# Reordering the hand-over from the output projection to the up projection

## The chip, the cores and the metric

The kernel runs on one core of one Trainium2 chip. The metric is the device time of one execution, in microseconds (us). Three runs of the kernel before gave 1262.51 to 1264.11 us, with a median of 1263.84 us.

## The reference

One decoder layer for 1024 tokens and a width of 1024, all in fp32:

```python
a = rmsnorm(h, g_mix[i]);  proj = a @ w_in[i]          # gated convolution and attention groups
h = h + jnp.concatenate([conv_out, attn], axis=-1) @ w_out[i]
m = rmsnorm(h, g_mlp[i])
h = h + jnp.square(jax.nn.relu(m @ w_up[i])) @ w_down[i]
gate = jax.nn.sigmoid(rmsnorm(h, g_ple[i]) @ w_ple_gate[i])
h = h + gate * (p[i] @ w_ple_proj[i]);  out = rmsnorm(h, g_final)
```

The change lies between the second line (the output projection, whose result is the new residual) and the fourth (`m @ w_up`, 1024 x 4096).

## The kernel before

**Number format.** Every fp32 operand of a matrix product is cut in two parts: *hi*, a cast on ScalarE (ACT, L904), and *lo*, the difference of operand and hi, a subtraction on VectorE (DVE, L908). A product takes three matmuls per 128-deep piece, in the order hi*hi, hi*lo, lo*hi. So the first matmul of a product needs only the hi part of the right operand, and the second needs its lo part.

**Output projection, second half.** Eight steps `tt`, one for each 128 tokens, with two halves of 512 columns each. `out_half(tt, dh)` records the 12 matmuls of one half (L158) and its *eviction*, the addition of the bank to the residual row on DVE (L725). A step also has: `norm_begin(tt)`, the sum of squares on ACT (L118) and two small instructions on GpSimd (POOL, L123 and L126) that give the row's factor `rs`; the store of the row to `h_d` by the SP queue; and, one step later, `m_row(tt)` (L1290), the normalised row, which waits for `rs`. Rows 0 to 3 of the normalised residual go out to `m_d` and come back in another layout (`row_back`, L1273), and four transposes on DVE (`turn_part`, L1279) put them into the four units of `turn_raw[0]`. Rows 4 to 7 are turned on TensorE (`turn_on_pe`, L1307), and ACT copies them (L1309) into `turn_raw[1]`.

**Up projection.** One level of a Strassen scheme. For each of 16 slabs `n` of 256 columns of `w_up` there are seven products, P1 to P7, of 12 matmuls each (L1016). Their right operands are blocks of the turned residual: P1 uses B11 and P2 uses B21 (the two halves of `turn_raw[0]`), P3 uses B22, and P5, P6, P7, P4 use the combinations T1 to T4, which DVE makes by subtraction (L842) before they are cut in hi and lo. The left operands of a slab are cut by `blocks_jobs` (for P1, P2, P4) and `sums_jobs` (for P5, P6, P7, P3). After its product, a bank goes through ACT: a copy into another bank (P1, L1046), a relu and a square (P2 and P4, L1021 and L1022), or a plain copy (P6 L1052, P7 L1056). With P2 to P4 the result goes to `hs_d`. In what follows, "P1(2)" is product P1 of slab 2.

**What sets the order.** Here PE, DVE, ACT and SP keep the order in which the code records their instructions. The cutting of operands is recorded as *jobs* in one queue. `pump(us)` adds `us` to a credit and runs jobs, each with a cost that the code states, while the credit is above zero; the credit never keeps more than 0.5. `begin_ahead` records the casts of the first two jobs of the queue early. Where a product's operand has not been cut yet, `up` runs jobs until it has:

```python
while name not in ups[n] or RIGHT[name] not in M:
    run_one()
```

Such *forced* jobs are recorded after everything that the product before put on ACT and DVE. Their costs are taken off the credit, so that the next pumps run fewer jobs.

Of the kernel before, what the change touches and what calls it, by code (L numbers as in the profile page):

```python
# [14 lines left out]
P = 128  # L15
# [46 lines left out]
def hybrid_layer_kernel(ctx: ExitStack, tc: tile.TileContext, x, p, g_mix, w_in, conv_w, g_conv_out,  # L62
                        g_attn_out, w_out, g_mlp, w_up, w_down, g_ple, w_ple_gate, w_ple_proj,
                        g_final, out):
    nc = tc.nc
    x, p, w_in, conv_w, w_out, w_up, w_down, w_gate, w_proj, out = (
        x[0], p[0, 0], w_in[0], conv_w[0], w_out[0], w_up[0], w_down[0], w_ple_gate[0], w_ple_proj[0], out[0])
# [639 lines left out]
    h1 = []  # L707
# [126 lines left out]
    def free(*us):  # L834
        for u in us:
            U.put(u, "W")
# [20 lines left out]
    jobs = deque()  # L857
# [20 lines left out]
    def begin_ahead():  # L878
        for j in list(jobs)[:AHEAD]:
            if j.act and (j.need is None or j.need.done) and len(U.free_q["W"]) > SPARE:  # L880
                j.begin()

    def run_one():
        j = jobs.popleft()
        j.begin()
        j.dve()
        j.done = True
        credit[0] -= j.cost
        begin_ahead()

    def pump(us):
        credit[0] += us
        begin_ahead()
        while jobs and credit[0] > 0:
            run_one()
        credit[0] = min(credit[0], 0.5)
# [41 lines left out]
    def sums_jobs(n, r, between=None):  # L938

        ops = ups[n]  # L940
        a11, a21 = r[0][0][:, :, 0:P], r[0][0][:, :, P:256]
        a12, a22 = r[1][0][:, :, 0:P], r[1][0][:, :, P:256]
        box = {}

        def s_sums():
            s = box["s"] = W(F32, (P, 2, 4, P))
            add(s[0][:, 0], a21, a22)
            sub(s[0][:, 1], s[0][:, 0], a11)

        def q_sums():  # L950
            q = box["q"] = W(F32, (P, 2, 4, P))
            sub(q[0][:, 0], a11, a21)
            sub(q[0][:, 1], a12, box["s"][0][:, 1])
            free(*r)

        made = {"s": job(s_sums, 1.4), "q": job(q_sums, 1.4)}
        if between:
            job(between, 0.0)
        for key, names in (("s", ("P5", "P6")), ("q", ("P7", "P3"))):
            def outs(key=key):  # L960
                box[key + "o"] = W(F32R, (P, 2, 4, P)), W(F32R, (P, 2, 4, P))
                return [u[0] for u in box[key + "o"]]

            def done(key=key, names=names):
                hi, lo = box[key + "o"]
                free(box[key])
                held = Held([hi, lo], 2)
                for i, name in enumerate(names):
                    ops[name] = ((lambda t, i=i: hi[0][:, i, t]), (lambda t, i=i: lo[0][:, i, t]), held)

            split_job(1.23, outs, lambda key=key: box[key][0], done, made[key])
# [3 lines left out]
    def block_jobs(name, raws_of, done=None, need=(None, None)):  # L975
        hi, lo = [], []
        for i in range(2):
            def outs():
                hi.append(W(F32R, (P, 2, HB)))
                lo.append(W(F32R, (P, 2, HB)))  # L980
                return hi[-1][0], lo[-1][0]

            def ready(i=i):
                if i == 1:
                    M[name] = ((lambda t: hi[t // 2][0][:, t % 2]), (lambda t: lo[t // 2][0][:, t % 2]), hi + lo)
                    if done:
                        done()
            split_job(1.23, outs, lambda i=i: raws_of()[i][0], ready, need[i])
# [44 lines left out]
    def up(n, name, us=2.6):  # L1033
# [54 lines left out]
        squares.extend(due)  # L1088
        if n == NP_ - 1:
            free(*M[RIGHT[name]][2])  # L1090
        pump(us)


    GP, NG = 2, NP_ // 2
# [166 lines left out]
    def out_half(tt, dh):  # L1261
        for _ in out_bank(y2, w2, tt, dh, TAGS[(2 * tt + dh) % 4]):
            pass
# [49 lines left out]
    with tc.manual_schedule(engines={mybir.EngineType.PE, mybir.EngineType.DVE, mybir.EngineType.Activation,  # L1313
# [2 lines left out]
        sums_jobs(1, raws[1])  # L1316
        for tt in range(8):
            out_half(tt, 0)
            if tt >= 1:
                m_row(tt - 1)  # L1320
            out_half(tt, 1)
            if 3 <= tt <= 6:
                if tt == 3:
                    turn_raw[0] += raw_units()
                turn_part(turn_raw[0], tt - 3, tt - 3, range(4))
            else:
                pump(3.6)
            norm_begin(h1, tt)
            nc.sync.dma_start(out=h_d[tt * P:(tt + 1) * P], in_=h1[tt][0])
            if 1 <= tt <= 4:  # L1330
                row_back(m_d, tt - 1)
            if tt == 6:
                while jobs:
                    run_one()
                r0 = turn_raw[0]
                block_jobs("B11", lambda: r0[0:2])
                block_jobs("B21", lambda: r0[2:4])
                begin_ahead()
        for a, b in y2 + w2:
            free(a, b)  # L1340
        blocks_jobs(2, raws[2])
        sums_jobs(2, raws[2])
        up(0, "P1", 2.4)
        m_row(7)
        free(grow)
        turn_on_pe(4)
        turn_on_pe(5)
        up(1, "P1", 2.6)
        turn_on_pe(6)
        turn_on_pe(7)  # L1350
        up(0, "P2", 0.0)
# [15 lines left out]
        t1, t2 = [], []  # L1367
        made = combine_jobs(sub, b12, b11, t1, lambda: free(*b11))
        block_jobs("T1", lambda: t1, need=made)
        made = combine_jobs(sub, b22, t1, t2, lambda: free(*t1))  # L1370
        block_jobs("T2", lambda: t2, need=made)
        t3 = list(b12)
# [280 lines left out]
```

## Time and profile before

| | |
|---|---|
| median of three runs | 1263.84 us |
| the profiled execution's own time | 1267.23 us |
| its span, first to last instruction | 1265.5 us |
| TensorE (PE) busy | 1213.4 us, 96% |
| DVE busy | 963.0 us, 76% |
| ACT busy | 628.5 us, 50% |
| mean granted TensorE clock | 0.986 |

All stretches below are microseconds from the start of the profiled span. Matmuls are pipelined and their ends are modelled, so the time of a product is read from start to start. An instruction's busy time on DVE or ACT overlaps that of the next by about 0.1 us.

### The profile page before, as it was taken

Reading aid. Unit: us, or ns where it says so; the run is one execution under the profiler, and the core shown is the slowest. Engines: PE = TensorE matmul, PEld = TensorE weight load, DVE = VectorE, ACT = ScalarE, POOL = GpSimd, SP = SyncE. Lnnn points to the kernel's source line nnn. Section 1 sums busy time; section 2 is a strip of 40 time slices with the busy share of each in tenths; the row PEclk is TensorE's granted clock in tenths of the full one; section 3 lists DMA queues with packets and bytes.
Section 4 is the critical chain, followed back from the end, with each engine's and each line's share of the span. In section 5 each row is a group of like instructions: output and inputs, shape, how many; then the busy total and the mean of one; then the engine's idle time right before and its main releaser. Section 6 shows DMA issues by size and latency. Waiting matters only on the chain.

```text
span 1265.5 us, 15613 instructions
## 1 busy us (share of the span) xinstructions
PE 1213.4 (96%) x5629; PEld 1004.0 (79%) x5629; DVE 963.0 (76%) x1367; ACT 628.5 (50%) x1049; POOL 236.4 (19%) x248
## 2 busy tenths in 40 slices
PE   8999999999998999899999999987899999999997
PEld 6788888878877788678888888865788888887786
DVE  3656898989989976678666766665889888886774
ACT  5445465555565432456545545563344444435543
POOL 3302544545448531000000000000000000002121
PEclk9999999999998999899999999989999999999899
DMA  9711011111122325124677776799787876567432
GB/s 361 221 34 44 28 31 34 35 34 34 34 67 89 128 81 203 66 92 164 231 271 251 262 276 249 276 302 325 243 258 228 264 239 214 190 207 229 134 101 99
DMA packets 152229, 209.71 MB, mean 166 GB/s; under 512 B 8004, under 2 KB 111448, under 8 KB 152152
## 3 DMA queue, kind: packets, MB, share of 16 engines
q1 hardware_dynamic: 151608, 207.67, 49.0%
q8 instruction: 44, 0.72, 0.2%
q10 hardware_dynamic: 544, 1.05, 0.2%
q14 instruction: 33, 0.27, 0.1%
HBM read 141.58 MB, written 67.11 MB: 165 GB/s over the span
## 4 chain that ended last, share of the span: by engine, by line
PE 51%; DVE 4%; DMA 3%; ACT 1%; issue 1%; SPq 0%; POOL 0%; POOLq 0%; DVEq 0%; ACTq 0%
PE ps_mm L1016 13%; PE ps_z L1016 12%; PE ps_av L1016 12%; PE ps_tr L1016 7%; PE ps_z L158 2%; PE ps_tr L158 2%; PE ps_mm L158 2%; PE ps_av L158 2%; DMA u<-hs_d 1%; DMA u<-h_d 1%; DVE u L1279 1%; DVE u L908 1%; DVE u L839 1%; DMA n_d<-u 1%; DVE u L842 1%
## 5 line engine op out<-in xcount | busy, mean ns | idle before, releaser
L158 PE MATMUL ps_mm<-u,u 128*128 128x512 f32 (+1 forms) x1464 | 366.4, 396 | 7.1 <-ACT u L904 2.6
L158 PEld LDWEIGHTS ps_mm<-u,u 128*128 128x128 f32 x1464 | 269.8, 190 | 62.3 <-ACT u L904 3.0
L908 DVE TENSOR_TENSOR u<-u,u 128x1024 fp32r<-128x1024 f32 (+2 forms) x214 | 231.2, 1101 | 43.1 <-ACT u L904 36.4
L904 ACT CAST u<-u 128x1024 fp32r<-128x1024 f32 (+2 forms) x214 | 195.0, 952 | 91.3 <-DVE u L842 20.4
L1016 PE MATMUL ps_z<-u,u 128*128 128x512 f32 x768 | 194.5, 396 | 14.4 <-DVE u L908 6.5
L1016 PE MATMUL ps_mm<-u,u 128*128 128x512 f32 x768 | 191.4, 391 | 6.5 <-DVE u L839 5.8
L1016 PE MATMUL ps_av<-u,u 128*128 128x512 f32 x744 | 186.1, 392 | 1.4 <-DVE u L908 1.4
L1016 PEld LDWEIGHTS ps_z<-u,u 128*128 128x128 f32 x768 | 145.9, 191 | 48.5 <-DVE u L908 8.3
L1016 PEld LDWEIGHTS ps_mm<-u,u 128*128 128x128 f32 x768 | 144.6, 189 | 38.2 <-DVE u L839 7.1
L1016 PEld LDWEIGHTS ps_av<-u,u 128*128 128x128 f32 x744 | 140.3, 189 | 31.8 <-DVE u L908 2.1
L123 POOL TENSOR_SCALAR me<-ms 128x1 f32<-128x1 f32 x24 | 10.3, 430 | 705.0 <-DVE u L839 619.6
L839 DVE TENSOR_TENSOR u<-ps_av,u 128x512 f32<-128x512 f32 x94 | 64.7, 689 | 81.8 <-PE ps_av L1016 48.1
L1016 PE MATMUL ps_tr<-u,u 128*128 128x512 f32 x408 | 102.0, 394 | 0.0
L1016 PEld LDWEIGHTS ps_tr<-u,u 128*128 128x128 f32 x408 | 77.6, 190 | 16.4
L603 POOL TENSOR_TENSOR u<-u,u 128x383 f32<-128x383 f32 (+5 forms) x72 | 72.7, 1012 | 94.4 <-DVE u L601 50.3
L842 DVE TENSOR_TENSOR u<-u,u 128x512 f32<-128x512 f32 (+1 forms) x120 | 84.2, 723 | 1.7
L620 ACT CAST u<-ps_tr 128x512 fp32r<-128x512 f32 (+1 forms) x80 | 43.5, 544 | 60.8 <-PE ps_tr L615 60.3
L645 PEld LDWEIGHTS ps_av<-u,u 128*128 128x128 f32 x320 | 50.2, 189 | 15.3 <-DVE u L621 9.0
L621 DVE TENSOR_TENSOR u<-ps_tr,u 128x512 fp32r<-128x512 f32 (+1 forms) x80 | 50.5, 632 | 14.8 <-ACT u L620 13.8
L596 DVE TENSOR_TENSOR_SCAN u<-u,floor 128x384 f32<-128x384 f32 (+2 forms) x64 | 58.4, 914 | 3.7 <-ACT u L588 3.6
L113 ACT CAST u<-u 128x1024 fp32r<-128x1024 f32 x42 | 43.9, 1054 | 33.9 <-DVE u L501 9.8
L645 PE MATMUL ps_av<-u,u 128*128 128x256 f32 (+1 forms) x320 | 52.9, 281 | 6.2 <-DVE u L621 6.1
(133 smaller groups left out, 1523.4 us busy)
## 6 DMA issues: line engine op xcount, KB each, us to landing
u<-in_w_down SPq DMA_DIRECT2D x56, 512.0 KB, 5.5
u<-hs_d SPq DMA_DIRECT2D x64, 448.0 KB, 5.8
hs_d<-u SPq DMA_DIRECT2D x48, 512.0 KB, 2.8
u<-in_w_up SPq DMA_DIRECT2D x32, 512.0 KB, 5.9
ws_d<-u SPq DMA_DIRECT2D x32, 512.0 KB, 2.8
u<-ws_d SPq DMA_DIRECT2D x32, 512.0 KB, 6.4
u<-in_w_in SPq DMA_DIRECT2D x24, 512.0 KB, 4.1
u<-in_x SPq DMA_DIRECT2D x16, 512.0 KB, 8.1
```

Of the source, the lines that this page charges most:

```text
L113: nc.scalar.copy(out=hi, in_=raw)
L158: nc.tensor.matmul(ps, a, b, start=(i == 0), stop=(i == n - 1))
L596: nc.vector.tensor_tensor_scan(out=rev, data0=rev, data1=floor[:, HB - (n - s0):][:, ::-1], initial=1.0, op0=ALU.mult, op1=ALU.max)
L603: (nc.vector if s0 > 0 and pr < 3 else nc.gpsimd).tensor_tensor(out=beta[:, s0:e], in0=beta[:, s0:e], in1=keep[:, s0 + 1:e + 1], op=ALU.mult)
L620: nc.scalar.copy(out=ah[:, :w], in_=tp[:, :w])
L621: nc.vector.tensor_tensor(out=al[:, :w], in0=tp[:, :w], in1=f32(ah[:, :w]), op=ALU.subtract)
L645: nc.tensor.matmul(av[:, t0:256], v, part[:, c0:c0 + 256 - t0], start=(j == 0 and part is ah), stop=(j == n - 1 and part is al))
L839: (eng or nc.vector).tensor_tensor(out=out, in0=a, in1=b, op=ALU.add)
L842: (eng or nc.vector).tensor_tensor(out=out, in0=a, in1=b, op=ALU.subtract)
L904: nc.scalar.copy(out=box["o"][0], in_=src())
L908: nc.vector.tensor_tensor(out=b, in0=src(), in1=f32(a), op=ALU.subtract)
L1016: nc.tensor.matmul(ps, a, b, start=(fresh and i == 0), stop=(i == n - 1), skip_group_check=not fresh)
```

## The change

It moves recorded instructions and changes none of them: the kernel after has the same instructions on each engine. Its parts:

1. In steps 3 to 6, the four transposes stand between the two evictions of a step, behind `m_row(tt - 1)`, instead of behind the second eviction.
2. The jobs of B11 and B21 are put at the head of the queue in step 6, before its second half, and the jobs that were left (the cutting of slab 1's sums) stay queued behind them. Before, those were all run first.
3. In step 7 two jobs (the lo parts of B11) run between the evictions, `m_row(6)` comes behind the second one, and `pump(3.6)` is gone.
4. The read of a turned row (`row_back`) is issued by SP ahead of the store of the step's residual row.
5. `up(1, "P1", None)` runs no pump behind P1(1).
6. `sums_jobs(2, ...)` is queued behind the jobs of T1 instead of ahead of them.

```diff
--- before.py
+++ after.py
@@ -1088,7 +1088,8 @@
         squares.extend(due)
         if n == NP_ - 1:
             free(*M[RIGHT[name]][2])
-        pump(us)
+        if us is not None:
+            pump(us)
 
 
     GP, NG = 2, NP_ // 2
@@ -1316,36 +1317,41 @@
         sums_jobs(1, raws[1])
         for tt in range(8):
             out_half(tt, 0)
-            if tt >= 1:
+            if tt == 7:
+                run_one()
+                run_one()
+            elif tt >= 1:
                 m_row(tt - 1)
-            out_half(tt, 1)
             if 3 <= tt <= 6:
                 if tt == 3:
                     turn_raw[0] += raw_units()
                 turn_part(turn_raw[0], tt - 3, tt - 3, range(4))
-            else:
+            if tt == 6:
+                r0 = turn_raw[0]
+                rest = list(jobs)
+                jobs.clear()
+                block_jobs("B11", lambda: r0[0:2])
+                block_jobs("B21", lambda: r0[2:4])
+                jobs.extend(rest)
+                begin_ahead()
+            out_half(tt, 1)
+            if tt == 7:
+                m_row(6)
+            if tt < 3:
                 pump(3.6)
             norm_begin(h1, tt)
-            nc.sync.dma_start(out=h_d[tt * P:(tt + 1) * P], in_=h1[tt][0])
             if 1 <= tt <= 4:
                 row_back(m_d, tt - 1)
-            if tt == 6:
-                while jobs:
-                    run_one()
-                r0 = turn_raw[0]
-                block_jobs("B11", lambda: r0[0:2])
-                block_jobs("B21", lambda: r0[2:4])
-                begin_ahead()
+            nc.sync.dma_start(out=h_d[tt * P:(tt + 1) * P], in_=h1[tt][0])
         for a, b in y2 + w2:
             free(a, b)
         blocks_jobs(2, raws[2])
-        sums_jobs(2, raws[2])
         up(0, "P1", 2.4)
         m_row(7)
         free(grow)
         turn_on_pe(4)
         turn_on_pe(5)
-        up(1, "P1", 2.6)
+        up(1, "P1", None)
         turn_on_pe(6)
         turn_on_pe(7)
         up(0, "P2", 0.0)
@@ -1367,6 +1373,7 @@
         t1, t2 = [], []
         made = combine_jobs(sub, b12, b11, t1, lambda: free(*b11))
         block_jobs("T1", lambda: t1, need=made)
+        sums_jobs(2, raws[2])
         made = combine_jobs(sub, b22, t1, t2, lambda: free(*t1))
         block_jobs("T2", lambda: t2, need=made)
         t3 = list(b12)
```

On DVE, steps 6 and 7 of the output projection (`u416` and `u417` are the residual rows 6 and 7, `u451` to `u454` the four units of `turn_raw[0]`, `u462` and later units of L1290/L1291 the normalised rows). Before:

```order
L725 TENSOR_TENSOR u416_4469<-ps_mm_4857,u416_4469 128x512
L1290 SCALAR_TENSOR_TENSOR u462_4871<-u396_4379,rs_4854,u429_4560 128x1024
L725 TENSOR_TENSOR u416_4469<-ps_z_4873,u416_4469 128x512
L1279 STREAM_TRANSPOSE u451_4746<-u459_4810 128x2x128
L1279 STREAM_TRANSPOSE u452_4747<-u459_4810 128x2x128
L1279 STREAM_TRANSPOSE u453_4748<-u459_4810 128x2x128
L1279 STREAM_TRANSPOSE u454_4749<-u459_4810 128x2x128
L908 TENSOR_TENSOR u444_4694<-u442_4690,u443_4693 128x1024
L908 TENSOR_TENSOR u447_4700<-u445_4696,u446_4699 128x1024
L725 TENSOR_TENSOR u417_4501<-ps_tr_4907,u417_4501 128x512
L1290 SCALAR_TENSOR_TENSOR u468_4921<-u416_4469,rs_4896,u429_4560 128x1024
L725 TENSOR_TENSOR u417_4501<-ps_av_4923,u417_4501 128x512
```

After:

```order
L725 TENSOR_TENSOR u416_4469<-ps_mm_4857,u416_4469 128x512
L1291 SCALAR_TENSOR_TENSOR u462_4871<-u396_4379,rs_4854,u429_4560 128x1024
L1280 STREAM_TRANSPOSE u451_4732<-u459_4809 128x2x128
L1280 STREAM_TRANSPOSE u452_4733<-u459_4809 128x2x128
L1280 STREAM_TRANSPOSE u453_4734<-u459_4809 128x2x128
L1280 STREAM_TRANSPOSE u454_4735<-u459_4809 128x2x128
L725 TENSOR_TENSOR u416_4469<-ps_z_4883,u416_4469 128x512
L725 TENSOR_TENSOR u417_4501<-ps_tr_4905,u417_4501 128x512
L908 TENSOR_TENSOR u464_4878<-u451_4732,u463_4877 128x1024
L908 TENSOR_TENSOR u466_4881<-u452_4733,u465_4880 128x1024
L725 TENSOR_TENSOR u417_4501<-ps_av_4924,u417_4501 128x512
L1291 SCALAR_TENSOR_TENSOR u470_4938<-u416_4469,rs_4902,u429_4560 128x1024
```

The transposes stand ahead of the eviction of row 6's second half (`ps_z`), and the two L908 that follow the eviction of `ps_tr` now make the lo parts of B11; the two L908 of slab 1's sums have gone further down.

On ACT, from the copy of P1(1)'s bank to the relu of P2(0) (`u432` and `u433` are slab 2 of `w_up`, `u475` to `u478` the units of `turn_raw[1]`). Before:

```order
L1046 COPY ps_tr_5015<-ps_mm_5002 128x512
L904 CAST u479_5018<-u432_4566 128x512
L904 CAST u480_5021<-u433_4567 128x1024
L1309 COPY u475_4970<-ps_av_5025 128x2x128
L1309 COPY u476_4971<-ps_av_5025 128x2x128
L1309 COPY u477_4972<-ps_av_5032 128x2x128
L1309 COPY u478_4973<-ps_av_5032 128x2x128
L1309 COPY u475_4970<-ps_av_5039 128x2x128
L1309 COPY u476_4971<-ps_av_5039 128x2x128
L1309 COPY u477_4972<-ps_av_5046 128x2x128
L1309 COPY u478_4973<-ps_av_5046 128x2x128
L1021 ACTIVATE u482_5065<-ps_tr_4966 128x512
```

After:

```order
L1046 COPY ps_tr_5013<-ps_mm_5000 128x512
L1310 COPY u475_4968<-ps_av_5015 128x2x128
L1310 COPY u476_4969<-ps_av_5015 128x2x128
L1310 COPY u477_4970<-ps_av_5022 128x2x128
L1310 COPY u478_4971<-ps_av_5022 128x2x128
L1310 COPY u475_4968<-ps_av_5029 128x2x128
L1310 COPY u476_4969<-ps_av_5029 128x2x128
L1310 COPY u477_4970<-ps_av_5036 128x2x128
L1310 COPY u478_4971<-ps_av_5036 128x2x128
L1021 ACTIVATE u479_5057<-ps_tr_4961 128x512
L1022 ACTIVATE u479_5057<-u479_5057 128x512
L904 CAST u482_5066<-u432_4566 128x512
```

The two casts of slab 2, which P1(2) and P2(2) read, stood ahead of the copies of rows 6 and 7 (`ps_av`); now the first of them stands behind the relu and the square of P2(0), and the second follows it.

On ACT, around the products P7 and P4 of slabs 0 to 2 (`u499` and `u502` hold T4, `u477` and `u478` hold B22, `u475` and `u476` hold T3). Before:

```order
L1052 COPY u491_5114<-ps_mm_5002 128x512
L904 CAST u509_5235<-u499_5160 128x1024
L904 CAST u511_5239<-u502_5178 128x1024
L1052 COPY u495_5136<-ps_z_5080 128x512
L904 CAST u513_5256<-u477_4972 128x1024
L904 CAST u515_5260<-u478_4973 128x1024
L1056 COPY u519_5279<-ps_z_4953 128x512
L1056 COPY u520_5295<-ps_mm_5002 128x512
L1021 ACTIVATE u519_5279<-u519_5279 128x512
L1022 ACTIVATE u519_5279<-u519_5279 128x512
```

After:

```order
L1052 COPY u486_5117<-ps_z_5073 128x512
L904 CAST u507_5242<-u476_4969 128x1024
L1056 COPY u511_5263<-ps_z_4948 128x512
L1056 COPY u512_5278<-ps_mm_5000 128x512
L1021 ACTIVATE u511_5263<-u511_5263 128x512
L1022 ACTIVATE u511_5263<-u511_5263 128x512
L904 CAST u513_5284<-u499_5186 128x1024
L904 CAST u515_5288<-u502_5191 128x1024
L1056 COPY u517_5303<-ps_z_5073 128x512
L1021 ACTIVATE u512_5278<-u512_5278 128x512
L1022 ACTIVATE u512_5278<-u512_5278 128x512
L904 CAST u518_5310<-u477_4970 128x1024
```

Before, the casts of T4 (`u509`, `u511`) are recorded before the copy of P6(2), and those of B22 (`u513`, `u515`) before the copies of P7. After, the casts of T4 (`u513`, `u515`) stand behind the copies of P7(0) and P7(1), and the first cast of B22 (`u518`) behind the copy of P7(2); the second one comes after the relu of P4(0).

## Rows read from the trace of the kernel before

**Rows 1.** PE timeline: start, busy us, engine, line, tiles, count, idle before, releaser.

```profile
514.71 0.39 PE L1016 MATMUL ps_z<-u,u 128*128 128x512 f32 x1
519.01 4.37 PE L1016 MATMUL ps_z<-u,u 128*128 128x512 f32 x11 [3.92 <-DVE u L908]
...
524.61 1.26 PE L1307 MATMUL ps_av<-ident,u 128*128 128x128 f32 x8 [0.34 <-ACT u L1309]
...
531.32 1.26 PE L1307 MATMUL ps_av<-ident,u 128*128 128x128 f32 x8 [1.81 <-ACT u L1309]
532.33 4.59 PE L1016 MATMUL ps_tr<-u,u 128*128 128x512 f32 x12
536.75 2.91 PE L1016 MATMUL ps_z<-u,u 128*128 128x512 f32 x12
...
544.95 0.40 PE L1016 MATMUL ps_av<-u,u 128*128 128x512 f32 x1
...
549.92 2.89 PE L1016 MATMUL ps_tr<-u,u 128*128 128x512 f32 x12
```

**Rows 2.** Windows view: stretch, length, busy of each engine, granted TensorE clock, DMA.

```profile
519.00:520.00 1.00, 0.99 (x2) 0.83 (x3) 1.00 (x1) 1.00 (x2) 0.82 (x1) 0.50 0.95 385
...
533.00:534.00 1.00, 1.00 (x4) 0.75 (x3) 1.00 (x3) 0.27 (x1) 0.00 (x0) 0.50 0.00 0
```

**Rows 3.** Windows view of two later stretches.

```profile
558.00:700.00 142.00, 142.00 (x629) 117.56 (x628) 99.20 (x132) 80.99 (x120) 0.00 (x0) 1.00 0.61 223
...
850.00:900.00 50.00, 37.19 (x149) 28.35 (x149) 33.26 (x44) 16.83 (x20) 0.00 (x0) 0.97 0.88 294
```

**Rows 4.** DVE timeline, 495 to 545.

```profile
495.19 1.28 DVE L1290 SCALAR_TENSOR_TENSOR u<-u,rs,u 128x1024 f32<-128x1024 f32 x1 [2.53 <-POOL rs L126]
...
505.59 0.70 DVE L725 TENSOR_TENSOR u<-ps_av,u 128x512 f32<-128x512 f32 x1
506.19 2.35 DVE L1279 STREAM_TRANSPOSE u<-u 128x256 f32<-128x256 f32 x4
...
508.97 1.33 DVE L1290 SCALAR_TENSOR_TENSOR u<-u,rs,u 128x1024 f32<-128x1024 f32 x1
...
513.01 2.42 DVE L908 TENSOR_TENSOR u<-u,u 128x1024 fp32r<-128x1024 f32 x2
...
517.64 2.45 DVE L908 TENSOR_TENSOR u<-u,u 128x1024 fp32r<-128x1024 f32 x2
...
542.41 2.35 DVE L842 TENSOR_TENSOR u<-u,u 128x1024 f32<-128x1024 f32 x2
```

**Rows 5.** ACT timeline, 506 to 547.

```profile
506.38 1.06 ACT L118 ACTIVATE u<-u 128x1024 f32<-128x1024 f32 x1 [3.45 <-issue]
...
529.15 1.57 ACT L904 CAST u<-u 128x512 fp32r<-128x512 f32 x2
...
536.96 0.60 ACT L1021 ACTIVATE u<-ps_tr 128x512 f32<-128x512 f32 x1 [3.69 <-PE ps_tr L1016]
537.59 0.63 ACT L1022 ACTIVATE u<-u 128x512 f32<-128x512 f32 x1
...
545.15 0.60 ACT L1021 ACTIVATE u<-ps_tr 128x512 f32<-128x512 f32 x1 [0.43 <-PE ps_tr L1016]
545.78 0.63 ACT L1022 ACTIVATE u<-u 128x512 f32<-128x512 f32 x1
546.32 1.03 ACT L904 CAST u<-u 128x1024 fp32r<-128x1024 f32 x1
```

**Rows 6.** POOL timeline, the factor of row 5.

```profile
507.91 0.55 POOL L126 TENSOR_TENSOR rs<-me,mhalf 128x1 f32<-128x1 f32 x1
```

**Rows 7.** Groups by form, 475 to 620: shapes, count, busy us, mean ns.

```profile
L908 DVE TENSOR_TENSOR u<-u,u 128x1024 fp32r<-128x1024 f32 x29 | 35.1, 1234 | 12.9 <-ACT u L904 12.0 <-DMA hs_d<-u 0.9
...
L904 ACT CAST u<-u 128x1024 fp32r<-128x1024 f32 x29 | 30.1, 1048 | 16.2 <-DVE u L842 14.8 <-issue 1.2
...
L1056 ACT COPY u<-ps_z 128x512 f32<-128x512 f32 x2 | 1.2, 586 | 0.4 <-PE ps_z L1016 0.4
```

## The prediction

> **What bounds the kernel now.** I read the windows first. From 558 to 700 us TensorE is busy all of 142 us with 629 matmuls at the full clock [rows 3], so 0.226 us each and 2.71 us for a product of 12; DVE and ACT have slack there. Time in this part of the kernel is therefore won or lost only where TensorE waits. Then the PE timeline over the hand-over. P1(0) begins at 514.71, and the seventh up product, P5(0), ends where P5(1) begins, at 549.92 [rows 1]. The reader is to see three kinds of loss in it. First, 3.92 us before the second matmul of P1(0), which waits for the lo part of B11 from DVE. Second, 0.34 and 1.81 us in the transposes, which wait for ACT's copies to free a bank. Third, P5(0): 544.95 to 549.92 is 4.97 us for a product of 2.71, so 2.26 us go to T1's hi and lo parts. The windows add a fourth: after the idle at 515 and after the one at 530 the granted clock is 0.50, the 1.2 GHz level [rows 2], and the product behind the second idle takes 532.33 to 536.75, 4.42 us, 1.7 more than at full speed [rows 1]. From 558 us on there is no wait [rows 3]. So the change can win some 12 us at most, and can lose wherever it makes a part late that is early now.
>
> The order of all instructions after is known; I carry the rows' durations forward through it. "Due" is when TensorE would reach a product without a wait.
>
> **A. The norm loop, and lo of B11.** With the transposes ahead of a step's second eviction, `m_row` of a row comes only one eviction after that row's own second eviction, and needs its `rs`. The trace has that chain: eviction at 505.59, sum of squares on ACT at 506.38 [rows 5], the last POOL instruction at 507.91 for 0.55 [rows 6], so `rs` is there 2.87 us after the eviction began. Before, the transposes and an eviction filled that time (`m_row` at 508.97, no idle [rows 4]); after, DVE waits. A round is 2.87 + 0.1 + 1.2 (`m_row`) + 2.25 (transposes) = 6.4 us against 5.4 of TensorE's. Three rounds from the `m_row` at 495.19 put the one of row 5 at 514.4 instead of 508.97; then 3.45 for it and its transposes, two evictions at 0.6, and lo of B11 at 1.23 [rows 7]: 520.3. Before, two L908 of slab 1's sums (513.01), two evictions and an `m_row` lay in front of it, and it ended near 518.85 (from 517.64) [rows 4]. So P1(0)'s second matmul is 1.3 us later, not earlier. The end of that product moves by 0 (if the half-clock stretch ends when it did) to 1.4: I take +0.7.
>
> **B. Rows 4 and 5 on TensorE.** ACT's cast for B21 now stands between the copy of P1(0)'s bank and the copies of row 4. The 0.34 us wait becomes about 1.3: +0.95, one cast [rows 7].
>
> **C. Rows 6 and 7.** Without the pump the two casts of slab 2 (529.15, 1.57 us [rows 5]) are no longer ahead of the copies. The wait of 1.81 falls to 0.34 as in the undisturbed pair: -1.5. No idle is left that halves P2(0)'s clock: -1.7. Together -3.2 (0 if another delay fills it).
>
> **D to J. Jobs that are now forced.** What slab 1's sums and the missing pumps paid off before is still in the queue when P2(0) comes, and by the code's own costs the products P2(0), P1(2), P5(0), P5(2), P6(0), P7(0), P4(0) and P3(0) each find their operand uncut; before, of these only P5(0) did, for one job. A forced cast is recorded behind the relu and square of the product before. From due, that costs 0.21 until the relu starts (536.75 [rows 1], 536.96 [rows 5]), 0.63 to the square, 0.54 to the next instruction (545.78 to 546.32 [rows 5]): 1.38 us before the cast begins.
>
> - D, P1(2): 1.38 + 0.6 (a 512-wide cast) = 2.0 idle, then a half-clock product (+1.7) in which lo costs another 0.2: +3.9. Before, it ran at 536.75 without a wait [rows 1].
> - E, P5(0): 1.38 + 1.05 (cast) + 1.23 (lo) = 3.7, less the first matmul, 3.5 idle; half clock for the rest of that stretch +1.2; less the 2.26 paid before: +2.4. That T1 comes ahead of slab 2's sums does not help, as its cast waits for P2(2)'s square.
> - F, P7(0): T3's second cast follows the copy of P6(2): 0.7 + 1.05 + 1.23 = 3.0 for the eighth matmul, due at 1.6: +1.4.
> - G, P4(0): T4's subtractions wait on DVE for the sum with P7(1)'s copy. P7(1) ends at due - 2.7; copy 0.59 [rows 7], sum 0.7, subtractions 2.35 (the row at 542.41 [rows 4]): due + 1.15. Then the second cast 1.05, the copy of P7(2) 0.55, its sum 0.7, lo 1.23: 4.7, so 4.4 idle, and 1.5 of half clock: +5.9.
> - H, P3(0): B22's second cast stands behind two relus and squares (1.38 + 1.26), cast 1.05, lo 1.23: 4.9 for the eighth matmul, due at 1.6: 3.35 idle, half clock 1.3: +4.65.
> - I, P1(3): lo of its left operand waits behind the sum with P3(0): +1.0.
> - J, P5(3): on DVE the lo of its left operand stands behind four sums of slab 1's result, and those wait for a square on ACT that ends 1.25 after due. 1.25 + 4 x 0.62 + 1.23 = 5.0 for the third matmul, due at 0.45: 4.6 idle, 1.8 of half clock: +6.4.
>
> A to C give -1.5, D to J +25.7: together +24. From slab 4 on the queue has caught up, the order on every engine is that of before, and TensorE is again bound by its own work, so the 24 us shift everything behind. The read of turned rows ahead of the residual's store costs nothing: the store queued behind it on SP is needed only when the down products load `h_d`, some 300 us on; without that cover it would cost one wait for `m_d`'s write, a few us. The profiled execution took 1267.23 us around a span of 1265.5, 3.4 above the median of the three runs; it becomes 1291, the median 1263.84 + 24 = **1288 us**.
>
> **Bounds.** The clock is 7.5 of the 24. If idles as short as these didn't lower it, +16.5; the 1.81 us idle did. If every one of the five costs the full 1.7, and C does not come true, +28.
>
> **A rule weighed.** That ACT holds a ready cast back is thin in the trace: ACT idled 0.43 us before P2(2)'s relu at 545.15, while the source of the cast at 546.32, subtracted from 542.41 on for 2.35, was just getting ready [rows 4, 5]. The Trainium skill, "TensorE: Matmul & The Clock Gate", section "Architectural detail: the array is 16× 32×32, not 1× 128×128", says ScalarE and VectorE take their instructions strictly first in, first out. That speaks against this change: by it all of D to J stands, +24; without it the casts would pass the relus and -1.5 would be left. The row goes with the rule, as far as 0.43 us can.
>
> **Rivals.**
> 1. *The casts find their place* (not slower). If on ACT and DVE the parts of slab 2, T1, T4 and B22 are done before their products are due, D to J fall away and A to C decide: -1.5, 1262. For it: ACT is busy 81 of 142 us in the stretch behind, so it has room [rows 3]. Against: the order itself puts each cast behind an instruction that reads the product just ended, and room does not help there. It decides from D to J below 1.5 us together.
> 2. *Half clock only after the two longest idles.* Then D, E and H lose their clock terms, 4 us or more, and +18 is left: 1282. For it, the 0.50 of the windows stands behind the longest idle, 3.92 us; against, it stands behind the one of 1.81 us too [rows 1, 2].
> 3. *The loss is given back later.* Between 850 and 900 TensorE is busy 37 of 50 us with DMA at 0.88 [rows 3]. If those 13 us are transfers that were triggered long before, a later TensorE finds them done: +12, 1276. Against: loads are issued by units that the same products free, so they shift too.
>
> **Chances.** The forecast 0.76; rival 2 0.12; rival 3 0.06; rival 1 0.06. The time is the forecast's, 1288. The range takes in rivals 2 and 3 and the upper bound, with 2 us more for what the durations carry: 1275 to 1294; it leaves out rival 1 and the tails. A measurement of this kernel can tell some 0.2%, 2.5 us, from no change. Rival 1 lies inside that, with an even chance to pass it on the fast side: faster 0.03, within 0.04, slower 0.93.
>
> **What would show it.** Right: on the PE timeline waits of about 2 us before P1(2) on ACT's L904, 2.5 and 0.8 in P5(0), over 3 in P4(0), 2.5 in P3(0), over 4 in P5(3), with a granted clock of 0.50 behind them; DVE's `m_row` waiting about 1.8 for POOL in steps 4 to 6; no wait of 1.8 between rows 6 and 7. Wrong: P1(2) to P5(3) back to back, or a loss at 570 to 610 that is gone by 900.

## The result, and the profile after

The kernel after takes 1292.37 us (median of four executions, 1290.2 to 1294.02) against 1263.97 us (four executions, 1262.51 to 1266.47) for the kernel before on the same chip. That is 28.4 us between the medians; the ratio is 1.0215, with a 95% interval of 1.0201 to 1.023, which makes 27.2 us. The profiled execution of after took 1290.2 us around a span of 1288.5, 23.0 more than that of before. TensorE (PE) has the same 5629 matmuls, and the granted clock falls from 0.986 to 0.979 on the mean.

The windows of after come first, the two that answer to [rows 3] being the second and the third.

```profile
500.00:625.00 125.00, 102.17 (x406) 79.14 (x405) 72.32 (x86) 54.01 (x86) 4.97 (x10) 0.92 0.27 97
...
625.00:800.00 175.00, 175.00 (x773) 144.91 (x773) 121.93 (x168) 93.87 (x142) 0.00 (x0) 1.00 0.70 257
...
825.00:925.00 100.00, 85.99 (x344) 67.60 (x343) 62.41 (x79) 45.88 (x60) 0.00 (x0) 0.93 0.85 286
```

The same of before, over the hand-over and over the stretch that corresponds to 825 to 925:

```profile
500.00:625.00 125.00, 117.50 (x514) 96.05 (x513) 91.08 (x111) 68.20 (x106) 3.87 (x8) 0.97 0.40 141
...
800.00:900.00 100.00, 84.04 (x342) 65.81 (x341) 61.98 (x78) 45.25 (x60) 0.00 (x0) 0.95 0.85 284
```

Between 500 and 625 us TensorE issued 406 matmuls where before issued 514. That is 108 x 0.226 = 24.4 us of work not yet done. The waits grew by 15.3 us of it (117.50 - 102.17), and the clock took some 7: from 505 to 630 us TensorE ran at 1.2 GHz for 20.5 us, before for 6.8, and half of the difference is lost. The last 2 us are busy time, too: ahead of a wait the last matmul counts as busy to its modelled end (0.50 us for the single one at 518.06), where within a product the next one starts after 0.226 us. After has 14 such waits in this stretch and before has 5.

Behind 625 the kernel is the old one: 175 of 175 us busy, and 86 of 100 us where before had 84. How much of the loss stays is read from the starts of the same matmul in both profiles. In after it starts 1.04 us later at 100 us already, far ahead of the change; from 625 to 820 us it starts 25.5 us later, at 900 us 24.95, and at the end 23.0. So 24.4 us arise in the hand-over. Of these 0.5 come back by 925, and 2.0 between the following two rows of after, which stand at 1164.57 and 1181.57 in before, where a product ran at half clock (experiment 12):

```profile
1189.50 4.24 PE L158 MATMUL ps_mm<-u,u 128*128 128x512 f32 x18
...
1204.57 5.60 PE L158 MATMUL ps_tr<-u,u 128*128 128x512 f32 x24
```

The PE timeline shows where (columns as in [rows 1]):

```profile
518.06 0.50 PE L1016 MATMUL ps_z<-u,u 128*128 128x512 f32 x1 [2.15 <-ACT u L904]
520.89 4.26 PE L1016 MATMUL ps_z<-u,u 128*128 128x512 f32 x11 [2.32 <-DVE u L908]
...
532.56 1.26 PE L1308 MATMUL ps_av<-ident,u 128*128 128x128 f32 x8 [0.35 <-ACT u L1310]
533.58 3.00 PE L1016 MATMUL ps_tr<-u,u 128*128 128x512 f32 x12
538.44 3.29 PE L1016 MATMUL ps_z<-u,u 128*128 128x512 f32 x12 [1.86 <-ACT u L904]
541.57 5.60 PE L1016 MATMUL ps_tr<-u,u 128*128 128x512 f32 x24
...
549.45 0.50 PE L1016 MATMUL ps_av<-u,u 128*128 128x512 f32 x1 [2.29 <-ACT u L904]
550.71 4.37 PE L1016 MATMUL ps_av<-u,u 128*128 128x512 f32 x11 [0.76 <-DVE u L908]
...
582.88 5.06 PE L1016 MATMUL ps_z<-u,u 128*128 128x512 f32 x11 [2.98 <-DVE u L908]
...
591.40 0.49 PE L1016 MATMUL ps_av<-u,u 128*128 128x512 f32 x1 [1.55 <-ACT u L904]
592.67 2.50 PE L1016 MATMUL ps_av<-u,u 128*128 128x512 f32 x5 [0.77 <-DVE u L908]
...
612.17 4.12 PE L1016 MATMUL ps_av<-u,u 128*128 128x512 f32 x10 [4.25 <-DVE u L908]
616.09 3.00 PE L1016 MATMUL ps_z<-u,u 128*128 128x512 f32 x12
```

P1(0) is at 518 to 525, and P2(0) at 533.58 runs at full speed now. Then come P1(2) at 538.44, P5(0) to 555, P4(0) at 582.88, P3(0) at 591 to 595 and P5(3) at 612.17: five products, of which before only P5(0) waited; P7(0) and P1(3) wait for 0.76 and 0.59 us. Four of the five have stretches below full clock right behind their waits, P1(2) alone has none:

```profile
552.00:553.00 1.00, 1.00 (x4) 0.76 (x3) 0.96 (x2) 0.00 (x0) 0.00 (x0) 0.50 0.00 0
...
584.00:586.00 2.00, 2.00 (x6) 1.55 (x5) 1.10 (x1) 0.00 (x0) 0.00 (x0) 0.50 0.00 0
...
592.00:594.00 2.00, 1.33 (x3) 1.14 (x4) 0.61 (x1) 0.00 (x0) 0.00 (x0) 0.59 0.00 0
...
614.00:616.00 2.00, 2.00 (x6) 1.61 (x5) 1.97 (x3) 0.00 (x0) 0.00 (x0) 0.50 0.17 66
```

On DVE, `m_row` of row 5 now comes at 515.10 and waits 1.61 us for its factor, where before it came at 508.97 with no idle [rows 4], and lo of B11 begins at 519.62 instead of 517.64. The two last rows are those ahead of P5(3): at 608.36 begins the first of four additions for slab 1's result, which waits for ACT's square, and only behind them, at 610.90, the L908 that P5(3)'s third matmul needs.

```profile
515.10 1.29 DVE L1291 SCALAR_TENSOR_TENSOR u<-u,rs,u 128x1024 f32<-128x1024 f32 x1 [1.61 <-POOL rs L126]
...
519.62 2.35 DVE L908 TENSOR_TENSOR u<-u,u 128x1024 fp32r<-128x1024 f32 x2
...
608.36 0.69 DVE L839 TENSOR_TENSOR u<-u,u 128x512 f32<-128x512 f32 x1 [0.51 <-ACT u L1022]
...
610.90 4.09 DVE L908 TENSOR_TENSOR u<-u,u 128x1024 fp32r<-128x1024 f32 x4
```

On ACT the casts stand behind a relu and a square; the last row here, POOL's, gives the factor that the `m_row` at 515.10 waits for and answers to [rows 6].

```profile
536.62 0.60 ACT L1021 ACTIVATE u<-ps_tr 128x512 f32<-128x512 f32 x1 [2.10 <-PE ps_tr L1016]
537.25 0.63 ACT L1022 ACTIVATE u<-u 128x512 f32<-128x512 f32 x1
537.78 1.55 ACT L904 CAST u<-u 128x512 fp32r<-128x512 f32 x2
...
587.98 0.60 ACT L1021 ACTIVATE u<-ps_z 128x512 f32<-128x512 f32 x1 [4.88 <-PE ps_z L1016]
...
590.32 1.55 ACT L904 CAST u<-u 128x1024 fp32r<-128x1024 f32 x2
...
514.51 0.55 POOL L126 TENSOR_TENSOR rs<-me,mhalf 128x1 f32<-128x1 f32 x1
```

The same casts of slab 2 were at 529.15 before [rows 5], ahead of the copies of rows 6 and 7. The two rows at 587.98 and 590.32 say most. The first cast at 590.32 reads the second unit of B22, which ACT itself had written some 55 us earlier, with the copies of row 7. ACT stood idle for 4.88 us, waited for the bank of P4(0), ran two relus and two squares and only then made the cast that P3(0) was waiting for. An instruction is not slower than it was [rows 7]; it only stands in another place:

```profile
L908 DVE TENSOR_TENSOR u<-u,u 128x1024 fp32r<-128x1024 f32 x29 | 34.5, 1221 | 18.7 <-ACT u L904 18.7
...
L904 ACT CAST u<-u 128x1024 fp32r<-128x1024 f32 x29 | 30.1, 1045 | 19.0 <-DVE u L842 15.8 <-DVE u L1280 2.8
```

### The profile page after: what moved, and what is told of

Read it like the earlier page. It is cut to its first block, busy times and chain, and to the rows that moved or that the text cites. A ratio compares the mean times of both kernels' runs of the same rounds, so it can differ in the third digit from the quotient of the medians.

```text
span 1288.5 us, 15609 instructions
## 1 busy us (share of the span) xinstructions
PE 1223.1 (95%) x5629; PEld 1008.3 (78%) x5629; DVE 962.5 (75%) x1367; ACT 628.7 (49%) x1049; POOL 237.6 (18%) x248
## 4 chain that ended last, share of the span: by engine, by line
PE 73%; DVE 12%; DMA 5%; issue 4%; ACT 3%; POOL 2%; SPq 1%; POOLq 0%; DVEq 0%; ACTq 0%
PE ps_mm L158 16%; PE ps_z L1016 12%; PE ps_mm L1016 12%; PE ps_av L1016 12%; PE ps_tr L1016 6%; PE ps_z L158 3%; PE ps_tr L158 3%; PE ps_av L158 3%; PE ps_av L645 2%; PE ps_tr L615 2%; PE ps_z L586 2%; DMA u<-h_d 1%; DVE u L601 1%; DVE u L908 1%; DVE u L621 1%
## 5 line engine op out<-in xcount | busy, mean ns | idle before, releaser
L158 PE MATMUL ps_mm<-u,u 128*128 128x512 f32 (+1 forms) x1464 | 366.9, 396 | 6.3 <-ACT u L200 2.1
L158 PEld LDWEIGHTS ps_mm<-u,u 128*128 128x128 f32 x1464 | 270.5, 190 | 61.2 <-ACT u L200 2.3
L908 DVE TENSOR_TENSOR u<-u,u 128x1024 fp32r<-128x1024 f32 (+2 forms) x214 | 230.4, 1099 | 48.3 <-ACT u L904 43.7
L1016 PE MATMUL ps_z<-u,u 128*128 128x512 f32 x768 | 199.1, 401 | 20.9 <-DVE u L908 8.4
L1016 PE MATMUL ps_av<-u,u 128*128 128x512 f32 x744 | 191.4, 400 | 9.6 <-DVE u L908 5.8
L1016 PEld LDWEIGHTS ps_av<-u,u 128*128 128x128 f32 x744 | 143.4, 193 | 42.0 <-DVE u L908 6.8
L645 PEld LDWEIGHTS ps_av<-u,u 128*128 128x128 f32 x320 | 50.2, 189 | 15.1 <-DVE u L621 8.9
L621 DVE TENSOR_TENSOR u<-ps_tr,u 128x512 fp32r<-128x512 f32 (+1 forms) x80 | 50.5, 632 | 14.9 <-ACT u L620 13.9
```

Source lines behind the costliest of these rows:

```text
L158: nc.tensor.matmul(ps, a, b, start=(i == 0), stop=(i == n - 1))
L621: nc.vector.tensor_tensor(out=al[:, :w], in0=tp[:, :w], in1=f32(ah[:, :w]), op=ALU.subtract)
L645: nc.tensor.matmul(av[:, t0:256], v, part[:, c0:c0 + 256 - t0], start=(j == 0 and part is ah), stop=(j == n - 1 and part is al))
L908: nc.vector.tensor_tensor(out=b, in0=src(), in1=f32(a), op=ALU.subtract)
L1016: nc.tensor.matmul(ps, a, b, start=(fresh and i == 0), stop=(i == n - 1), skip_group_check=not fresh)
```

## The experiments

All ratios are to the kernel before, run on the same chip in the same rounds. Gains and losses in us are worked out from the ratios, so they can differ by about 1 us from the difference of the medians.

**1. After, with the credit given back.** One line, behind the product P2(0):

```diff
         up(0, "P2", 0.0)
+        credit[0] = 3.0
```

> The kernel after with one line more, and nothing moved by hand: behind P2(0) the credit of the job queue is set to 3.0, about what the two missing pumps would have left. Theory T (the missing credit makes the operands of P1(2) to P5(3) be cut only when the products ask for them, and their casts then stand behind the relus): D to J are gone but for the wait before P1(2), A to C stay: -3 to +3 us against before. Rival N (the norm loop of part 1 makes everything behind it late): nothing changes, +20 to +28. Rival F (slab 1's sums, left in the queue by part 2, are the work too many): they are still in the queue, so +20 to +28.

1266.71 us against 1265.74, ratio 1.0009 (0.9998 to 1.0019). From 540 us on there is no wait left, where after had 14.9 us of them:

```profile
538.22 4.78 PE L1016 MATMUL ps_z<-u,u 128*128 128x512 f32 x12 [1.85 <-ACT u L904]
...
540.00:625.00 85.00, 85.00 (x370) 70.19 (x369) 64.92 (x78) 50.85 (x72) 0.00 (x0) 0.98 0.43 154
```

The instructions are the same, and so are the moves of parts 1 to 6; only the jobs behind P2(0) are recorded earlier. The wait before P1(2) stays: the relu and the square of P2(0), behind which its cast stands on ACT, are recorded ahead of the line. So terms E to J have one cause: the queue is behind when P2(0) begins, and 3 us of credit are enough to catch up.

**2. After, without part 1.** The second eviction (with `m_row(6)` in step 7) goes back ahead of the transposes; the jobs of B11 and B21 still enter the queue in step 6.

```diff
+            out_half(tt, 1)
+            if tt == 7:
+                m_row(6)
             if 3 <= tt <= 6:
...
-            out_half(tt, 1)
-            if tt == 7:
-                m_row(6)
```

> The kernel after with part 1 undone: the four transposes stand behind a step's second eviction again (and the jobs of B11 and B21 are queued behind them). Theory T: DVE no longer waits for the factor of the row, P1(0)'s second matmul comes about 3 us earlier, but D to J stay: +15 to +21 us against before, with waits before P4(0) and P5(3) as in the kernel after. Rival N: the loss is gone, 0 or faster.

1287.79 us, ratio 1.0172 (1.0142 to 1.0202), some 22 us, 1 us above the range that was expected. P1(0) has no wait (its 12 matmuls begin at 516.84 and the next row at 519.66), and the late ones are as in after. The clock is not: behind the same 2.28 and 0.76 us in P5(0) it stayed at full speed, 11 matmuls in 2.81 us where after took 4.37:

```profile
547.09 2.81 PE L1016 MATMUL ps_av<-u,u 128*128 128x512 f32 x11 [0.76 <-DVE u L908]
...
578.98 4.37 PE L1016 MATMUL ps_z<-u,u 128*128 128x512 f32 x11 [2.98 <-DVE u L908]
...
606.50 4.15 PE L1016 MATMUL ps_av<-u,u 128*128 128x512 f32 x10 [4.25 <-DVE u L908]
```

The place of the transposes costs some 6 us in P1(0) and has nothing to do with the late waits.

**3. After, without part 6.**

```diff
         blocks_jobs(2, raws[2])
+        sums_jobs(2, raws[2])
         up(0, "P1", 2.4)
...
-        sums_jobs(2, raws[2])
```

> The kernel after with part 6 undone: slab 2's sums are queued ahead of T1 again. Theory T: P5(0) now has to force the sums too before it gets T1, 4 to 5 us more than the kernel after has there: +24 to +31 us against before. Rival S (putting T1 ahead of the sums is what breaks the order): the loss is mostly gone, under +8.

1301.05 us, ratio 1.0269 (1.024 to 1.0297), 34 us, 3 us above the range that was expected. The 4 to 5 us more in P5(0) came: with slab 2's sums ahead of T1 it waits 6.89 us instead of 2.29. The miss is the prediction's, which held T1's place to be indifferent because its cast waits for P2(2)'s square anyway:

```profile
555.88 0.80 PE L1016 MATMUL ps_av<-u,u 128*128 128x512 f32 x1 [6.89 <-ACT u L904]
```

So part 6 helps, and without it the whole change would be worse by some 6 us. What the prediction says under E of T1's place is wrong.

**4. After, with the left jobs run at once in step 6**, as before.

```diff
-                rest = list(jobs)
-                jobs.clear()
+                while jobs:
+                    run_one()
...
-                jobs.extend(rest)
```

> The kernel after with the second half of part 2 undone: the jobs left of slab 1 are run in step 6 as before, and not kept in the queue. Theory T: running them early costs credit as well, so the later products still find their operands uncut; +19 to +25 us against before, and P1(0) later still, as the two subtractions stand ahead of B11's on DVE (wait of 4 to 5 us in P1(0)). Rival F: with those two jobs out of the queue D to J are gone, under +6.

1291.61 us, ratio 1.0203 (1.0184 to 1.0222), 25.7 us, just above what was expected. The wait before P1(2) is gone, but P1(0) now waits for slab 1's sums, and the late waits stay:

```profile
523.98 4.54 PE L1016 MATMUL ps_z<-u,u 128*128 128x512 f32 x11 [4.59 <-DVE u L908]
...
612.58 4.14 PE L1016 MATMUL ps_av<-u,u 128*128 128x512 f32 x10 [4.25 <-DVE u L908]
```

The jobs that part 2 leaves in the queue are not what makes the later ones late.

**5. After, with both pumps back.**

```diff
-            if tt < 3:
+            if tt < 3 or tt == 7:
                 pump(3.6)
...
-        up(1, "P1", None)
+        up(1, "P1", 2.6)
```

> The kernel after with both pumps back (3.6 in step 7, 2.6 behind P1(1)), all else as after. Theory T: D to J are gone; with the pump behind P1(1) the casts of slab 2 stand ahead of the copies of rows 6 and 7 again, so C's 1.8 us wait returns: -4 to +2 us against before, and no wait over 1 us behind P2(0). Rivals N and F: parts 1 and 2 are untouched, +15 or more.

1262.62 us against 1264.3, ratio 0.9985 (0.9973 to 0.9996). The idle between rows 6 and 7 is back, at 1.81 us, and there is none behind P2(0):

```profile
530.54 1.26 PE L1308 MATMUL ps_av<-ident,u 128*128 128x128 f32 x8 [1.81 <-ACT u L1310]
```

Two calls that run jobs make a difference of some 29 us between a kernel with and one without them. Together with 1 and 4 this settles it: the credit that the missing pumps no longer give is the cause. How the loss divides between the two pumps it does not say.

**6. Before, with part 5 alone.**

```diff
-        up(1, "P1", 2.6)
+        up(1, "P1", None)
```

> The kernel before with part 5 alone: no pump behind P1(1). Theory T: the wait of 1.81 us before rows 6 and 7's copies and the half-clock P2(0) are gone (-3 us), and the missing 2.6 of credit comes back as a longer wait in P5(0) (3.2 instead of 2.3 us, and a lowered clock): -1 to +4 us against before, no gain over 0.2%. Rival (one missing pump is enough to break the whole sequence): +10 or more. Rival (the pump only cost time): -3 us.

1266.44 us, ratio 1.0015 (1.0005 to 1.0025), 1.9 us. The removed pump does what it looks like between rows 6 and 7 (0.35 for 1.81), and the price appears in P5(0), with 0.9 us more between 572 and 582 (P3(0) to P1(3)):

```profile
527.35 1.26 PE L1308 MATMUL ps_av<-ident,u 128*128 128x128 f32 x8 [0.35 <-ACT u L1310]
...
542.57 0.51 PE L1016 MATMUL ps_av<-u,u 128*128 128x512 f32 x1 [3.04 <-ACT u L904]
```

With this one pump missing the queue has nearly caught up after one product; with both it has not until P5(3).

**7. Before, with part 6 alone.** The same move as in 3, the other way.

```diff
-        sums_jobs(2, raws[2])
         up(0, "P1", 2.4)
...
         block_jobs("T1", lambda: t1, need=made)
+        sums_jobs(2, raws[2])
```

> The kernel before with part 6 alone: T1 ahead of slab 2's sums. Theory T: with the credit of before T1's parts are ready when P5(0) is due, and its 2.26 us of waits go: -3 to -1 us against before. Rival S (the new order is bad by itself): slower by 2 us or more.

1262.15 us, ratio 0.9984 (0.9975 to 0.9994), 2.0 us faster: P5(0) has no wait, and the idle of 1.81 is the last one of the hand-over.

```profile
530.40 1.26 PE L1307 MATMUL ps_av<-ident,u 128*128 128x128 f32 x8 [1.81 <-ACT u L1309]
```

**8. A version built from these.** After, without part 1 (as in 2), with the pump of step 7 kept, the pumps of steps 0 to 2 and 7 moved behind `norm_begin`, and the pump of P1(1) moved behind the transposes of row 7:

```diff
-            if tt < 3:
-                pump(3.6)
             norm_begin(h1, tt)
+            if tt < 3 or tt == 7:
+                pump(3.6)
...
         turn_on_pe(7)
+        pump(2.6)
         up(0, "P2", 0.0)
```

> The parts that the rows favour, with the credit kept: transposes behind the second eviction as before, B11's jobs ahead of slab 1's sums, the pump of step 7 kept, the pump behind P1(1) moved behind the copies of rows 6 and 7, T1 ahead of slab 2's sums; and in each step the sum of squares recorded ahead of the pump's casts, so that m_row(2) no longer waits 2.5 us for its factor. Theory T: the wait in P1(0) falls from 3.9 to about 1.3 us, that of 1.8 to 0.3, P5(0)'s 2.3 to 0, and no half-clock stretch is left: -12 to -6 us against before. Rival (waits only move on to the next product, as DVE has no room): -3 to +3.

1254.47 us (1253.89 to 1257.32), ratio 0.9928 (0.9915 to 0.994): 9.1 us faster than before, and by the two ratios some 36 faster than after. Two idles are left between 500 and 625 us, and the clock in that window is 1.00:

```profile
518.88 1.26 PE L1308 MATMUL ps_av<-ident,u 128*128 128x128 f32 x8 [1.29 <-ACT u L1310]
...
500.00:625.00 125.00, 123.36 (x558) 102.39 (x557) 94.45 (x114) 73.48 (x114) 5.17 (x7) 1.00 0.46 162
```

The idea of the change, lo of B11 earlier and the casts out of the way of the copies, is worth 9 us in this version, in which no credit is taken out of the queue and the transposes stay behind both evictions. What the pumps' place behind `norm_begin` adds to it was not run alone.

**9. Before, with part 1 alone.**

```diff
-            out_half(tt, 1)
             if 3 <= tt <= 6:
...
-            else:
+            out_half(tt, 1)
+            if not 3 <= tt <= 6:
                 pump(3.6)
```

> The kernel before with part 1 alone: transposes between a step's two evictions, all else as before. The norm loop of 6.3 us a step makes DVE late, and with slab 1's two subtractions, m_row(6) and an eviction still ahead of B11's lo parts the wait in P1(0) grows from 3.9 to about 6, and that in the transposes from 0.3 to about 3: +3 to +9 us against before, and P5(0) no worse than before, as the credit is that of before. Rival (the loop is hidden by TensorE's own work): -1 to +1.

1271.22 us against 1264.87, ratio 1.0045 (1.0031 to 1.0059), 5.7 us. The norm chain delays the hi part of B11, and the jobs of slab 1's sums, which this kernel still runs in step 6, stand ahead of its lo part as in 4. P1(0) waits 8.45 us in all, where about 6 were expected; the wait in the transposes, expected at about 3, stays at 0.33:

```profile
518.56 0.79 PE L1016 MATMUL ps_z<-u,u 128*128 128x512 f32 x1 [5.36 <-ACT u L904]
522.44 4.87 PE L1016 MATMUL ps_z<-u,u 128*128 128x512 f32 x11 [3.09 <-DVE u L908]
```

**10. Before, with part 4 alone.** The lines of `row_back` go ahead of the store of the residual row.

```diff
-            nc.sync.dma_start(out=h_d[tt * P:(tt + 1) * P], in_=h1[tt][0])
             if 1 <= tt <= 4:
                 row_back(m_d, tt - 1)
+            nc.sync.dma_start(out=h_d[tt * P:(tt + 1) * P], in_=h1[tt][0])
```

> The kernel before with part 4 alone: the read of the turned row issued ahead of the residual's store. Nothing that any engine waits for moves: -1 to +1 us against before. Rival (the store, now later, delays a transfer that matters): +1 to +4.

1265.8 us, ratio 1.0004 (0.9992 to 1.0015): nothing, as said.

**11. After, once more with a profile.**

> The kernel after once more, for its clock: the same waits at the same places as in its first profile (13 idles over 0.5 us, within 0.3 us of those but for one or two). If the executions differ by the clock, this one has another count of stretches at 1.2 GHz behind the waits than the six of 3.4 us in the first profile, and its span differs by about 1.7 us for each.

1292.59 us, span 1290.9, clock 0.977. The waits over 0.5 us stand at the same places, and two of them differ in length: 0.76 us for 1.28 before row 5's transposes, 2.10 for 1.55 in P3(0). What differs most is the clock: in 505 to 630 us TensorE ran at 1.2 GHz for 27.3 us in all, two stretches of 3.4 us more than in the first profile. At 1.7 us each that would make the span 3.4 us longer; it is 2.4 longer. Behind the same 1.86 us before P1(2) it kept 2.4 GHz there (538.44 to 541.57) and lost it here:

```profile
538.05 4.87 PE L1016 MATMUL ps_z<-u,u 128*128 128x512 f32 x12 [1.86 <-ACT u L904]
542.73 5.67 PE L1016 MATMUL ps_tr<-u,u 128*128 128x512 f32 x24
...
617.77 2.94 PE L1016 MATMUL ps_z<-u,u 128*128 128x512 f32 x12
```

**12. Before, once more with a profile.**

> The kernel before, unchanged, once more with a profile: the median of after stands 28 us above the median of before, while the two profiled executions stand 23.0 apart, and the one of before was 3.3 us above its own median. Theory (the clock): this execution takes 1262 to 1265 us, and TensorE spends less time at 1.2 GHz between 505 and 630 us than the 6.8 us of the first profile, or less elsewhere; waits over 0.5 us stand in the same places (3.9 in P1(0), 1.8 between rows 6 and 7, 2.3 in P5(0)). Rival (the profiled execution of before is always above): 1266 to 1268 us again, with the same clock.

1265.73 us, span 1264.0, clock 0.989: between what the two theories gave, so neither is borne out. The 29 executions of before beside experiments 5 to 8 took 1262.08 to 1268.23 us, so that neither this one nor the 1267.23 of the first profile stands out. In the hand-over this execution is the first one over again (6.8 us at 1.2 GHz, P5(1) at 549.71 against 549.92). It differs far behind: between 825 and 900 us it loses 1.0, and most at the start of the L158 products behind the down projection. Here it waits 1.83 and 0.59 us and keeps the clock:

```profile
1171.41 0.73 PE L158 MATMUL ps_mm<-u,u 128*128 128x512 f32 x2 [1.83 <-ACT u L904]
1172.73 1.20 PE L158 MATMUL ps_mm<-u,u 128*128 128x512 f32 x4 [0.59 <-DVE u L908]
...
1179.24 5.60 PE L158 MATMUL ps_tr<-u,u 128*128 128x512 f32 x24
```

In the first profile of before the wait was 2.62 us, with a product at half clock behind it:

```profile
1171.44 3.38 PE L158 MATMUL ps_mm<-u,u 128*128 128x512 f32 x6 [2.62 <-ACT u L904]
...
1181.57 5.60 PE L158 MATMUL ps_tr<-u,u 128*128 128x512 f32 x24
```

The same product of 24 begins at 1179.24 and at 1181.57, though the 18 matmuls ahead of the wait had begun 0.8 us later here (1165.34 for 1164.57): 3.1 us for one place, in a part of the kernel that the change does not touch. Behind it, 0.85 of them are lost again.

## Why the prediction was right

The time (1288 forecast, 1292.37 measured) lies inside the range of 1275 to 1294, near its upper end: two of the four executions touch it. By terms, each read from start to start against the first profile of before, with the 1.04 us (first) and -0.17 us (second profile of after) taken off by which the last half of the output projection began later or earlier (511.99 before, 513.03 and 511.82 after):

| term | forecast | first profile | second |
|---|---|---|---|
| A, norm loop and P1(0) | +0.7 | +0.73 | +1.48 |
| B, rows 4 and 5 | +0.95 | +0.94 | +0.98 |
| C, rows 6, 7 and P2(0) | -3.2 | -3.15 | -3.14 |
| D, P1(2) | +3.9 | +2.5 | +4.1 |
| E, P5(0) | +2.4 | +2.95 | +2.8 |
| F, P7(0) | +1.4 | +1.6 | +1.6 |
| G, P4(0) | +5.9 | +6.7 | +5.85 |
| H, P3(0) | +4.65 | +4.5 | +3.7 |
| I, P1(3) | +1.0 | +1.27 | +3.4 |
| J, P5(3) | +6.4 | +6.2 | +6.15 |
| sum, at the start of P4(2) | +24 | +24.3 | +27.2 |

In the second profile, 0.26 us of the sum lie in P5(1), which begins at 1.2 GHz, and belong to no row. That the first sum meets the forecast to 0.3 us is partly luck: D's 1.4 us too few are made up by E and G.

- **A** was right in size and only half right in its rows. `m_row` waited 1.6 us for POOL, near the 1.8 forecast, but P1(0) waits at two places, 2.15 us for hi and 2.32 for lo, where the forecast had one wait for lo. Experiment 2 takes it away alone, and 9 shows it alone.
- **B and C** hold to the tenth: 1.28 us before row 5's transposes, 0.35 between rows 6 and 7, P2(0) at 533.58 in 3.00 us. Experiment 6 repeats C in the kernel before.
- **D** is a wait of 1.86 us where 2.0 was said. The half clock behind it came in one execution and not in the other, which is nearly the whole error of the term.
- **E to H and J** hold to 0.95 us or better in both profiles, G with its parts shifted: it waits 0.90 and 2.98 us where 4.4 was said, and the clock behind takes some 2.4 us in the first profile and 1.6 in the second, for 1.5. They were put down to forced jobs, and experiment 1 shows it: the credit back, and all five are gone with no instruction changed. Experiment 5 shows that it is the two pumps that were missing, and 4 that it is not the unflushed queue.
- **E's side remark** is the step that failed: that T1 ahead of slab 2's sums does not help. Experiments 7 and 3 show that its place is worth 2 us in the kernel before and some 6 in after. It did not touch the sum, since the waits of E were worked out with the order that after has.
- **I** was mis-sized in the second execution: +3.4, as the lower clock from 594 to 601 lay on it.
- **Part 4** costs nothing (experiment 10).

Of the rivals, the first (the casts find their place, 1262) falls by the rows at 536.62 and 587.98: ACT was idle for 2.10 and for 4.88 us, and the cast behind came no earlier. This is what the rule of the Trainium skill says that was weighed ("TensorE: Matmul & The Clock Gate", section "Architectural detail: the array is 16× 32×32, not 1× 128×128"): strictly first in, first out. The 0.43 us that the trace of before had for it was thin; 4.88 us before a cast whose source is 55 us old is not, though no row shows whether the unit that this cast writes was free as long. The third rival falls by the starts behind 820: the waits over 0.5 us sum up to 14.0 us in 825 to 925 and to 15.6 in 800 to 900 of before, and the same matmul starts 25.5 us later ahead of this stretch and 24.95 behind it. So 0.5 of the 24 came back.

The second rival, half clock only behind the longest idles, falls as it was put: after the 2.98 us of P4(0) and the 4.25 of P5(3) the clock fell every time, but after 2.29 and 0.76 in P5(0) as well, in both profiles of after and in experiment 4. Its price was also off: the clock terms of D, E and H add up to 4.2, which leaves 19.8 and not 18. But it had seen something. In experiment 2 the clock stayed up behind the waits of P5(0) and of P3(0) (2.08 and 0.77). Behind a wait of 1.81 to 1.86 us the clock fell in both executions of before, in experiments 1 to 3 and in 11, and did not in after's first profile nor in experiments 5, 7, 9 and 10. The prediction counted it as certain.

That leaves the size. The sums of the two profiles are 24.3 and 27.2, the medians 28.4 apart (27.2 by the ratio). The single executions of after lie at 1290.2, 1290.73, 1294.01 and 1294.02, and the two profiles show one way in which such a gap of 3 us comes about. On the side of before, experiment 12 shows 3.1 us from one wait behind 1165. How much of the 28.4 is such chance in either kernel, and whether the waits of the change make it worse elsewhere, stays open.

Taken alone, part 1 costs 5.7 us, part 4 nothing, part 5 1.9, and part 6 gains 2.0: 5.6 together, of 27. Parts 2 and 3 weren't run alone. Most of the loss belongs to no single part of these but goes when both pumps are back. Whether it takes both of them missing, or the pump of step 7 alone (part 3's) would do it, was not tried and stays open.

## What to carry to other kernels

Where a queue of jobs is paid out by credit, a removed pump costs nothing where it stood: it shifts later jobs to the point at which they are forced, behind the last instruction that reads the product before, and there an idle engine doesn't help. So move a pump rather than delete it (experiment 5: both put back, 29 us; experiment 8: one moved past the copies that it disturbed, as a part of 9 us won). And before such a change, go through the order of the engines for each product that finds its operand uncut, and add up relu, square, cast and lo from the rows of the trace: here this gave ten terms, of which nine came out within 1 us in the first profile, nine in the second, and eight in both.

## What the runs showed of the hardware

The same wait, of 1.86 us at the same product of the same program, was followed by 2.4 GHz in one execution and by 1.2 GHz in the next (538.44 and 538.05). The same pair of waits in P5(0), 2.28 and 0.76 us, was followed by 1.2 GHz in both profiles of after and by 2.4 GHz in experiment 2 (547.09). Behind waits of 1.3 us and less standing by themselves, as the 1.29 of experiment 8, the clock stayed at 2.4 GHz. A wait near 2 us has to be priced with both outcomes, 0 and some 1.6 us.
